# Weight sums on multiples of 128 bytes, plain chunks first and fifth, an eighth product group per layer in a decoder trunk

## The chip, the cores and the metric

The kernel runs on one core of a Trainium2 chip. The metric is the device time of one execution in microseconds (us). The engines that matter here are PE (TensorE, matrix products), DVE (VectorE) and ACT (ScalarE). Nearly all data lie in the on-chip memory SBUF, 128 partitions wide, and a tile's place is its byte offset within a partition. A difference of 0.2% is 4 us.

## The reference

The reference is a two-layer decoder trunk on 256 tokens of width 2048 in float32. What bears on the change is the feed-forward block, once in each layer:

```
D_MODEL = 2048
SEQ = 256
D_FF = ((8 * D_MODEL // 3 + 255) // 256) * 256   # 5632

def swiglu_ffn(x, g, w_in, w_out):
    h = rms_norm(x, g)
    gate, up = jnp.split(h @ w_in, 2, axis=-1)
    return x + (jax.nn.silu(gate) * up) @ w_out
```

Around it stand a recurrent block (layer 0) and a shared key/value projection with a sliding-window attention (layer 1), which the change leaves as they are but for where their tiles lie.

## The kernel before

**Three products for one.** Each float32 operand is held as two rounded parts, a high and a low one, and a product is the sum of high x high, high x low and low x high, each at PE's single-pass rate. Activations are held so in work tiles `s`; model weights arrive by DMA in `raw` (128 x 1024) and are split into `hi` (by ACT, line 311) and `lo` (by DVE, line 312). Four buffers of each rotate. One such tile is a *chunk*: 256 input features by 512 output features. `stream` (line 337) runs over all chunks: at chunk i it issues the load of chunk i+4, the split of chunk i+3, and the matmuls of chunk i.

**Stationary and moving.** A matmul first loads a 128 x 128 stationary operand into the array and then streams a moving operand of 256 or 512 columns past it. In the profile's rows `out<-in,in` the first input is the moving one and the second the stationary one.

**Direct groups.** `group` (line 362) takes 512 output features over all 2048 input features: 8 chunks of 24 matmuls on line 358, each with the model weight (`hi` or `lo`) stationary and 256 activation columns (`s`) moving: `b<-s,hi`. In the groups that are given `sync`, some chunks have three matmuls with 512 moving columns in place of six with 256.

**Fast groups.** A feed-forward block's input product has 22 groups (g = 0 to 21). Groups 0 to 4 are direct, and so are those from 18 on; groups 5, 7, ..., 17 (`FAST`) are *fast* ones, in `fast_group` (line 502), and the even ones between are direct. In a fast group the activations are stationary and the model weights move (`b<-hi,s`). Six of its eight chunks (`PAIRS`: 0, 1, 2, 4, 5, 6) are computed with seven block products in place of eight: 21 matmuls in place of 24. Three of the seven products use the weights as they are: 9 matmuls with `hi` or `lo` moving. The other four use sums of weight blocks, which `mix` (line 314) makes on DVE and ACT, three chunks ahead, in the work tiles `mh` and `ml`: 12 matmuls with a work tile moving, `b<-s,s`. The other two chunks are plain. Chunk 7 has 24 matmuls of 256 columns. Chunk 3 (`RUNS`) has nine of 512 and six of 256: three wide ones, a narrow one, three wide ones, a narrow one, three wide ones, four narrow ones. Ahead of chunk 3, `flush` issues what the fast group before left over: four transposes on line 711.

**The end of a block.** The group after the last fast one (g = 18) is direct with `sync` in chunks 0, 3, 4 and 5 and with the last flush ahead of chunk 3; behind it, a background task (`split`, in `ffn`) begins to split the 22 gated products into high and low parts for the output product, whose 88 chunks are all direct.

**What sets the order.** Each engine runs its instructions in the order of the program. A run-ahead planner (`run_bg`, with budgets in ns for DVE and ACT) only decides between which chunks the background pieces are issued.

**Where tiles lie.** All work tiles are of 4096 bytes and come from a rotating list of 30 (`whole`, `double`). Tiles are laid out in the order of their creation, each rounded up to 32 bytes: 16,384 bytes of DMA scratch, 128 bytes of constants, `par` (1096 bytes), `con` (4104), `cc` (128), `x`, `raw`, `hi`, `lo`, `t`, `h` (multiples of 1024), two `rstd` (1032 each), `acc`, two `sq` (1024 each), `zero` (1536), and then the work tiles. So `raw`, `hi` and `lo` begin at multiples of 128 bytes, and the two `rstd` (1056 bytes each with the rounding, 2112 together, which is 64 more than a multiple of 128) put all work tiles 64 bytes past such a multiple. In the following "at 0" and "at 64" stand for the offset modulo 128. All slices that a matmul takes begin a multiple of 512 bytes into their tile, so they are at 0 or 64 as the tile is.

Of the kernel before, what the change touches and what calls it, by code (L numbers as in the profile page):

```python
# [12 lines left out]
F32 = mybir.dt.float32  # L13
F32R = mybir.dt.float32r
# [3 lines left out]
P = 128  # L18
D = 2048
T = 256  # L20
# [15 lines left out]
K_ONE, K_BLK, K_SEL0, K_SEL1, K_ID = 0, 128, 256, 384, 512  # L36
K_HS, K_MASK = 640, 642
NCON = 642 + 384


class Val:
# [7 lines left out]
class Trunk:  # L49
# [10 lines left out]
    DEBT = 2500.0  # L60
    SYNC = (0, 2, 5)
    PLAIN = 4
    FAST = tuple(range(5, 18, 2))
    PAIRS = (0, 1, 2, 4, 5, 6)
    RUNS = 3
    OWED = 9000.0
    MORE = 2800.0
    WARM = 30
# [3 lines left out]
    def __init__(self, ctx, tc, dram):  # L72
        self.tc, self.nc, self.d = tc, tc.nc, dram
        nc = self.nc
        const = ctx.enter_context(tc.tile_pool(name="const", bufs=1))
        psum = ctx.enter_context(tc.tile_pool(name="psum", bufs=1, space=bass.MemoryType.PSUM))
        tmp = ctx.enter_context(tc.tile_pool(name="tmp", bufs=1))
        self.tmp = tmp
        self.par = const.tile([P, NPAR], F32, name="par")
        self.con = const.tile([P, NCON], F32, name="con")  # L80
        self.cc = const.tile([P, 32], F32, name="cc")
        self.x = [const.tile([P, 4, T], F32, name=f"x{i}") for i in range(4)]
        self.whole = deque((i, 0) for i in range(30))
        self.stamp = 0
        self.part = {F32: deque(), F32R: deque()}
        self.spool = const
        self.held = {}
        self.raw = [const.tile([P, 1024], F32, name=f"raw{i}") for i in range(4)]
        self.hi = [const.tile([P, 1024], F32R, name=f"hi{i}") for i in range(4)]
        self.lo = [const.tile([P, 1024], F32R, name=f"lo{i}") for i in range(4)]  # L90
# [4 lines left out]
        self.tmps = deque(const.tile([P, T], F32, name=f"t{i}") for i in range(4))  # L95
        self.halves = deque(const.tile([P, T], F32, name=f"h{i}") for i in range(4))
        self.rstd = [const.tile([P, T + 2], F32, name=f"rstd{i}") for i in range(2)]
        self.acc = const.tile([P, T], F32, name="acc")
        self.sq = deque(const.tile([P, T], F32, name=f"sq{i}") for i in range(2))
        self.zero = const.tile([P, P + T], F32R, name="zero")  # L100
# [41 lines left out]
        self.nc.vector.reciprocal(out, a)  # L142


    def double(self, dt=F32R):
        i, _ = self.whole.popleft()
        s = self.spool.tile([P, 4 * T], dt, tag=f"s{i}", name=f"s{i}")
        self.held[id(s)] = (i, s)
        return s

# [163 lines left out]
    def mix(self, i, raw, hi, lo):  # L314

        act, tt = self.nc.scalar.activation, self.nc.vector.tensor_tensor
        d = self.double(F32)
        mh, ml = self.double(), self.double()
        two = lambda ap: ap.rearrange("p (a c) -> p a c", c=T)
        q = slice(T, 4 * T)  # L320
        act(hi[:, q], raw[:, q], AF.Copy)  # L321
        tt(two(d[:, 0:2 * T]), two(raw[:, T:3 * T]), raw[:, 0:T].unsqueeze(1).to_broadcast([P, 2, T]), ALU.subtract)  # L322
        tt(d[:, 2 * T:3 * T], raw[:, 2 * T:3 * T], d[:, 0:T], ALU.add)
        tt(d[:, 3 * T:4 * T], raw[:, 3 * T:4 * T], d[:, 2 * T:3 * T], ALU.subtract)  # L324
        act(mh[:, :], d[:, :], AF.Copy)  # L325
# [179 lines left out]
    def fast_group(self, src, xn, mx, g, done, final):  # L505
# [10 lines left out]
        def plain(c, hi, lo):  # L516
# [732 lines left out]

    def run(self):  # L1250
        nc, d = self.nc, self.d
        const = self.tmp
        self.nm = const.tile([P, T + 2], F32, name="nm")
        self.nt = const.tile([P, T + 2], F32, name="nt")
        self.r2 = const.tile([P, 2], F32, name="r2")
        self.rrs = [const.tile([P, 48], F32, name=f"rr{i}") for i in range(2)]
# [90 lines left out]
```

## Time and profile before

| | |
|---|---|
| time, median of 3 runs | 1994.03 us (1992.72 to 1994.22) |
| the profiled execution | 1994.55 us, its span 1992.4 us |
| DVE, ACT busy | 1458.5 us (73%), 1123.0 us (56%) |
| DMA | 376.56 MB, mean 189 GB/s |
| granted PE clock | 1.00 in every stage |
| direct matmuls, line 358 | 12,807 |
| fast-group matmuls, line 512 | 2310: 1008 with a work tile moving, 1302 with `hi` or `lo` |

The profile comes from one profiled execution. "Busy" of PE is a union of modelled spans that overlap, so a PE that is busy all the time says only that it never ran dry, not that it goes at its best rate. That rate is read from the timeline: each row has the start of a run of like matmuls, the time to the end of its last, and their number, and the difference of the starts of two rows, divided by the number of matmuls between them, is the *pitch*, the time that one matmul takes in the stream.

### The profile page before, as it was taken

How to read it: one execution, taken by the hardware profiler on the slowest of the kernel's cores; microseconds unless marked ns; L12 is line 12 of the kernel's file. 1: busy time of each engine (PE TensorE's matmuls, PEld its weight loads, DVE VectorE, ACT ScalarE, POOL GpSimd, SP SyncE). 2: the span in 40 equal slices, each digit the busy share in tenths (PEclk: the TensorE clock that was granted, in tenths of full speed). 3: DMA queues.
4: the chain of work that ended last, by engine and by line, in shares of the span. 5: the costliest groups of instructions: out<-in, count | busy, mean ns of one | idle time of the engine just before them, and what ended most of it. 6: DMA issues, size and time to landing. Idle time of an engine off the chain costs nothing. (4 is left out here: it accounts for less than half of the span.)

```text
span 1992.4 us, 39949 instructions
## 1 busy us (share of the span) xinstructions
PE 1982.9 (100%) x16487; PEld 1935.5 (97%) x16487; DVE 1458.5 (73%) x2319; ACT 1123.0 (56%) x1626; POOL 0.2 (0%) x4
## 2 busy tenths in 40 slices
PE   9999999999999999999999999999999999999999
PEld 9999999999999999999998789999999999999999
DVE  8989868788888955555677776697888888444543
ACT  7788756555555744444556775564555556444342
POOL 0000000000000000000000000000000000000000
PEclk9999999999999999999999999999999999999999
DMA  7555655655566565555554334565655655556663
GB/s 267 194 188 180 201 191 180 202 198 194 199 201 199 196 196 197 191 191 201 192 181 154 111 128 150 189 191 190 203 201 196 198 196 197 187 190 204 208 202 128
DMA packets 105015, 376.56 MB, mean 189 GB/s; under 512 B 11648, under 2 KB 13824, under 8 KB 104832
## 3 DMA queue, kind: packets, MB, share of 16 engines
q1 hardware_dynamic: 104544, 373.60, 56.6%
q8 instruction: 129, 2.11, 0.4%
q14 instruction: 54, 0.44, 0.1%
q10 hardware_dynamic: 288, 0.40, 0.1%
HBM read 371.86 MB, written 2.10 MB: 188 GB/s over the span
## 5 line engine op out<-in xcount | busy, mean ns | idle before, releaser
L358 PE MATMUL b<-s,hi 128*128 128x256 f32 (+1 forms) x8455 | 1128.5, 280 | 1.6 <-ACT s L118 1.2
L312 DVE TENSOR_TENSOR lo<-raw,hi 128x1024 fp32r<-128x1024 f32 (+1 forms) x621 | 755.9, 1220 | 435.7 <-ACT hi L311 421.2
L358 PEld LDWEIGHTS b<-s,hi 128*128 128x128 f32 x8455 | 1051.7, 188 | 14.2 <-ACT s L118 2.0
L311 ACT ACTIVATE hi<-raw 128x1024 fp32r<-128x1024 f32 (+1 forms) x621 | 654.2, 1056 | 590.5 <-PE b L358 475.0
L358 PE MATMUL b<-s,lo 128*128 128x256 f32 x4352 | 647.1, 277 | 0.0
L358 PEld LDWEIGHTS b<-s,lo 128*128 128x128 f32 x4352 | 564.7, 188 | 0.1
L512 PE MATMUL b<-hi,s 128*128 128x256 f32 (+1 forms) x868 | 163.0, 292 | 0.0
L325 ACT ACTIVATE s<-s 128x1024 fp32r<-128x1024 f32 x84 | 89.2, 1062 | 108.6 <-DVE s L324 107.8
L512 PEld LDWEIGHTS b<-hi,s 128*128 128x128 f32 x868 | 130.4, 189 | 3.8
L512 PE MATMUL b<-s,s 128*128 128x256 f32 x1008 | 133.3, 281 | 0.0
L512 PEld LDWEIGHTS b<-s,s 128*128 128x128 f32 x1008 | 125.2, 189 | 0.0
L327 DVE TENSOR_TENSOR s<-s,s 128x1024 fp32r<-128x1024 f32 x84 | 102.7, 1222 | 20.1 <-ACT s L325 19.9
L512 PE MATMUL b<-lo,s 128*128 128x256 f32 (+1 forms) x434 | 114.1, 289 | 0.0
L118 ACT ACTIVATE s<-s 128x512 fp32r<-128x512 f32 (+3 forms) x172 | 83.0, 519 | 18.4 <-DVE s L127 13.1
L321 ACT ACTIVATE hi<-raw 128x768 fp32r<-128x768 f32 x84 | 70.3, 843 | 35.1 <-issue 21.8
L1232 PE MATMUL b<-hi,s 128*128 128x512 f32 x256 | 84.0, 408 | 0.0
L326 DVE TENSOR_TENSOR lo<-raw,hi 128x768 fp32r<-128x768 f32 x84 | 79.9, 951 | 0.0
L512 PEld LDWEIGHTS b<-lo,s 128*128 128x128 f32 x434 | 76.4, 188 | 1.8
L127 DVE TENSOR_TENSOR s<-s,s 128x512 fp32r<-128x512 f32 (+2 forms) x143 | 74.0, 549 | 4.4 <-ACT s L118 4.4
L322 DVE TENSOR_TENSOR s<-raw 128x512 f32<-128x512 f32 x84 | 57.7, 686 | 12.4 <-DMA raw<-in_ffn_in 12.3
L118 ACT ACTIVATE s<-b 128x256 fp32r<-128x256 f32 (+4 forms) x112 | 49.9, 480 | 25.9 <-PE b L1128 7.9
L1232 PEld LDWEIGHTS b<-hi,s 128*128 128x128 f32 x256 | 45.8, 189 | 9.6 <-issue 1.4
(117 smaller groups left out, 1098.6 us busy)
## 6 DMA issues: line engine op xcount, KB each, us to landing
raw<-in_ffn_in SPq DMA_DIRECT2D x352, 512.0 KB, 3.3
raw<-in_ffn_out SPq DMA_DIRECT2D x176, 512.0 KB, 3.3
raw<-in_lru_in SPq DMA_DIRECT2D x63, 512.0 KB, 3.8
raw<-in_lru_out SPq DMA_DIRECT2D x32, 512.0 KB, 3.4
raw<-in_w_q SPq DMA_DIRECT2D x32, 512.0 KB, 3.2
raw<-in_w_o SPq DMA_DIRECT2D x32, 512.0 KB, 3.3
raw<-in_gate SPq DMA_DIRECT2D x8, 512.0 KB, 4.0
raw<-in_kv SPq DMA_DIRECT2D x8, 512.0 KB, 3.2
```

The lines of the kernel that those rows point to most:

```text
L118: self.nc.scalar.activation(out, in_, func, **kw)
L127: self.nc.vector.tensor_tensor(out, a, b, op)
L311: self.nc.scalar.activation(hi[:, q], raw[:, q], AF.Copy)
L312: self.nc.vector.tensor_tensor(lo[:, q], raw[:, q], hi[:, q].bitcast(F32), ALU.subtract)
L321: act(hi[:, q], raw[:, q], AF.Copy)
L322: tt(two(d[:, 0:2 * T]), two(raw[:, T:3 * T]), raw[:, 0:T].unsqueeze(1).to_broadcast([P, 2, T]), ALU.subtract)
L325: act(mh[:, :], d[:, :], AF.Copy)
L326: tt(lo[:, q], raw[:, q], hi[:, q].bitcast(F32), ALU.subtract)
L327: tt(ml[:, :], d[:, :], mh[:, :].bitcast(F32), ALU.subtract)
L358: self.nc.tensor.matmul(ps[f][:, 0:c1 - c0], w, x2[k][:, c0:c1], start=f not in begun, stop=last and all(q[1] != f for q in todo[n + 1:]))
L512: nc.tensor.matmul(st["ps"][b][:, h % 2 * T:(h % 2 + n) * T], x, w, start=b not in st["begun"], stop=True, skip_group_check=True)
L1232: nc.tensor.matmul(st[g][b][:, :], x, q, start=c + kt == 0 and x is xh and q is wh, stop=c == 7 and kt == 1 and q is wl)
```

## The change

There are four edits.

- Groups 5, 7, ..., 19 are fast: eight in each layer. The groups behind (20, 21) are direct, and `sync`, the last flush and the start of `split` go with group 20.
- The plain chunks of a fast group are 0 and 4, both in the form with wide matmuls, and chunks 1, 2, 3, 5, 6, 7 use seven products. The flush stands ahead of chunk 4.
- The work tiles get 64 bytes more each, their list has 33, and `double` places a tile within them: `mh` and `ml` at 0, all others at 64, as before.
- The small tiles are laid out anew (a pad of 608 bytes, one more `sq` that serves as `acc`), and the DMA scratch is 2048 bytes.

```diff
+PAD = 152
...
-    FAST = tuple(range(5, 18, 2))
-    PAIRS = (0, 1, 2, 4, 5, 6)
-    RUNS = 3
+    FAST = tuple(range(5, 20, 2))
+    PAIRS = (1, 2, 3, 5, 6, 7)
+    RUNS = (0, 4)
...
-        self.whole = deque((i, 0) for i in range(30))
+        const.tile([P, PAD], F32, name="pad")
+        self.sq = deque(const.tile([P, T], F32, name=f"sq{i}") for i in range(3))
+        self.acc = self.sq.popleft()
+        self.whole = deque((i, 0) for i in range(33))
...
-    def double(self, dt=F32R):
+    def double(self, dt=F32R, place=64):
         i, _ = self.whole.popleft()
-        s = self.spool.tile([P, 4 * T], dt, tag=f"s{i}", name=f"s{i}")
+        o = (place // 64 + i) % 2 * 16
+        s = self.spool.tile([P, 4 * T + 16], dt, tag=f"s{i}", name=f"s{i}")[:, o:o + 4 * T]
...
-        mh, ml = self.double(), self.double()
+        mh, ml = self.double(place=0), self.double(place=0)
...
-            if c == self.RUNS:
+            if c in self.RUNS:
                 n = narrow(wide[3]) + narrow(wide[4]) + narrow(wide[5])
                 todo = sum(map(full, wide[0:3]), []) + n[0:1] + sum(map(full, wide[6:9]), []) + n[1:2]
                 todo += sum(map(full, wide[9:12]), []) + n[2:]
...
-                if c == self.RUNS:
+                if c == self.RUNS[1]:
                     self.flush()
...
-    nc = bacc.Bacc("TRN2", target_bir_lowering=False, num_devices=1)
+    nc = bacc.Bacc("TRN2", target_bir_lowering=False, num_devices=1, dynamic_dma_scratch_size=2048)
```

Two places on PE show the order. The first is where a direct group ends and the first fast group begins (`hi` and `lo` are of the chunk, `s` are work tiles, the outputs are PSUM banks). Before:

```order
L358 MATMUL b_86<-s_4432,hi_78 128x256 x2
L358 MATMUL b_86<-s_4432,lo_82 128x256
L512 MATMUL b_89<-hi_75,s_3900 128x256 x2
L512 MATMUL b_89<-lo_79,s_3900 128x256
L512 MATMUL b_88<-hi_75,s_3900 128x256 x2
L512 MATMUL b_88<-lo_79,s_3900 128x256
L512 MATMUL b_88<-hi_75,s_3929 128x256 x2
L512 MATMUL b_88<-lo_79,s_3929 128x256
L512 MATMUL b_90<-s_4742,s_3929 128x256 x2
L512 MATMUL b_90<-s_4743,s_3929 128x256
```

And with the change:

```order
L362 MATMUL b_103<-s_4397,hi_84 128x256 x2
L362 MATMUL b_103<-s_4397,lo_88 128x256
L516 MATMUL b_105<-hi_81,s_3898 128x512 x2
L516 MATMUL b_105<-lo_85,s_3898 128x512
L516 MATMUL b_104<-hi_81,s_3898 128x256
L516 MATMUL b_105<-hi_81,s_3898 128x512 x2
L516 MATMUL b_105<-lo_85,s_3898 128x512
L516 MATMUL b_104<-hi_81,s_3898 128x256
L516 MATMUL b_104<-hi_81,s_3898 128x512 x2
L516 MATMUL b_104<-lo_85,s_3898 128x512
L516 MATMUL b_104<-hi_81,s_3898 128x256 x2
L516 MATMUL b_104<-lo_85,s_3898 128x256 x2
```

The group now begins with the plain chunk in wide matmuls, and the first seven-product chunk, with its sums of weights, follows as the second.

The second place is around the flush in the second fast group (`con` holds the identity for the transposes). Before, the rows from the end of chunk 2 to the beginning of chunk 4:

```order
L512 MATMUL b_87<-s_5283,s_4028 128x256
L711 MATMUL b_85<-con,s_5064 128x128 x4
L512 MATMUL b_88<-hi_78,s_4144 128x512 x2
L512 MATMUL b_88<-lo_82,s_4144 128x512
L512 MATMUL b_87<-hi_78,s_4144 128x256
L512 MATMUL b_88<-hi_78,s_4144 128x512 x2
L512 MATMUL b_88<-lo_82,s_4144 128x512
L512 MATMUL b_87<-hi_78,s_4144 128x256
L512 MATMUL b_87<-hi_78,s_4144 128x512 x2
L512 MATMUL b_87<-lo_82,s_4144 128x512
L512 MATMUL b_87<-hi_78,s_4144 128x256 x2
L512 MATMUL b_87<-lo_82,s_4144 128x256 x2
```

With the change, the rows from the end of chunk 3:

```order
L516 MATMUL b_104<-s_5303,s_4059 128x256
L715 MATMUL b_102<-con,s_5053 128x128 x4
L516 MATMUL b_105<-hi_81,s_4174 128x512 x2
L516 MATMUL b_105<-lo_85,s_4174 128x512
L516 MATMUL b_104<-hi_81,s_4174 128x256
L516 MATMUL b_105<-hi_81,s_4174 128x512 x2
L516 MATMUL b_105<-lo_85,s_4174 128x512
L516 MATMUL b_104<-hi_81,s_4174 128x256
L516 MATMUL b_104<-hi_81,s_4174 128x512 x2
L516 MATMUL b_104<-lo_85,s_4174 128x512
L516 MATMUL b_104<-hi_81,s_4174 128x256 x2
L516 MATMUL b_104<-lo_85,s_4174 128x256 x2
```

The flush and the wide chunk are the same instructions in the same order as before; they have moved one chunk back, and three seven-product chunks stand ahead of them and three behind.

More of the change, by code (lines that the diff above doesn't have):

```diff
@@ L76, in __init__ @@
         psum = ctx.enter_context(tc.tile_pool(name="psum", bufs=1, space=bass.MemoryType.PSUM))
-        tmp = ctx.enter_context(tc.tile_pool(name="tmp", bufs=1))
-        self.tmp = tmp
         self.par = const.tile([P, NPAR], F32, name="par")
@@ L81, in __init__ @@
         self.cc = const.tile([P, 32], F32, name="cc")
-        self.x = [const.tile([P, 4, T], F32, name=f"x{i}") for i in range(4)]
-        self.whole = deque((i, 0) for i in range(30))
+        self.rstd = [const.tile([P, T + 2], F32, name=f"rstd{i}") for i in range(2)]
+        self.nm, self.nt = (const.tile([P, T + 2], F32, name=n) for n in ("nm", "nt"))
+        self.r2 = const.tile([P, 2], F32, name="r2")
+        self.rrs = [const.tile([P, 48], F32, name=f"rr{i}") for i in range(2)]
+        self.zero = const.tile([P, P + T], F32R, name="zero")
+        const.tile([P, PAD], F32, name="pad")
+        self.x = [const.tile([P, 4, T], F32, name=f"x{i}") for i in range(4)]
+        self.raw = [const.tile([P, 1024], F32, name=f"raw{i}") for i in range(4)]
+        self.hi = [const.tile([P, 1024], F32R, name=f"hi{i}") for i in range(4)]
+        self.lo = [const.tile([P, 1024], F32R, name=f"lo{i}") for i in range(4)]
+        self.tmps = deque(const.tile([P, T], F32, name=f"t{i}") for i in range(4))
+        self.halves = deque(const.tile([P, T], F32, name=f"h{i}") for i in range(4))
+        self.sq = deque(const.tile([P, T], F32, name=f"sq{i}") for i in range(3))
+        self.acc = self.sq.popleft()
+        self.whole = deque((i, 0) for i in range(33))
         self.stamp = 0
@@ L87, in __init__ @@
         self.held = {}
-        self.raw = [const.tile([P, 1024], F32, name=f"raw{i}") for i in range(4)]
-        self.hi = [const.tile([P, 1024], F32R, name=f"hi{i}") for i in range(4)]
-        self.lo = [const.tile([P, 1024], F32R, name=f"lo{i}") for i in range(4)]
         self.sets = [[psum.tile([P, 512], F32, name=f"b{4 * i + j}") for j in range(4)] for i in range(2)]
@@ L94, in __init__ @@
         self.started = False
[L95 to L100, printed above, removed]
         self.jobs = []
@@ L1251, in run @@
         nc, d = self.nc, self.d
[L1252 to L1256, printed above, removed]
         self.rv = {i: Val() for i in range(4)}
```

## The prediction

> **What bounds the kernel now.** I read the page's busy times first, then those of single stages, then the PE timeline.
>
> ```profile
> PE 1982.9 (100%) x16487; PEld 1935.5 (97%) x16487; DVE 1458.5 (73%) x2319; ACT 1123.0 (56%) x1626; POOL 0.2 (0%) x4
> ```
>
> PE is busy throughout. The stages below are one fast group with its flush, the direct group behind it, and the output product of the last layer; the columns are the stage, its length, and busy PE, PEld, DVE, ACT and POOL, then granted clock and DMA.
>
> ```profile
> 452.19:472.99 20.80, 20.80 (x172) 20.40 (x171) 17.49 (x25) 11.91 (x16) 0.00 (x0) 1.00 0.63 207
> 472.99:494.75 21.76, 21.76 (x195) 21.76 (x193) 18.97 (x27) 11.30 (x12) 0.00 (x0) 1.00 0.56 190
> 1755.00:1992.00 237.00, 234.36 (x2044) 233.16 (x2042) 109.64 (x105) 89.79 (x89) 0.00 (x0) 1.00 0.57 187
> ```
>
> PE never runs dry in the groups, the granted clock is 1.00, and DVE, the next engine, has 36.46 us of work in a pair of groups of 42.56 us. So the time is the number of matmuls times their pitch. A direct group of 192 matmuls takes 21.76 us, 113 ns each.
>
> The pitch is not one number. The key/value stage alternates twelve direct matmuls (line 1038, work tile at 64 moving, weights at 0 stationary) with twelve in the roles of a fast group (lines 1047 to 1049, weights moving). These are the starts of five such dozens:
>
> ```profile
> 1012.94 0.39 PE L1038 MATMUL b<-s,hi 128*128 128x256 f32 x2
> ...
> 1014.30 0.28 PE L1047 MATMUL b<-hi,s 128*128 128x256 f32 x1
> ...
> 1015.72 0.40 PE L1038 MATMUL b<-s,hi 128*128 128x256 f32 x2
> ...
> 1017.13 0.28 PE L1047 MATMUL b<-hi,s 128*128 128x256 f32 x1
> ...
> 1018.50 0.39 PE L1038 MATMUL b<-s,hi 128*128 128x256 f32 x2
> ```
>
> The differences over 12 are 113, 118, 118 and 114 ns. The shapes are the same, so the stream has two states, **short** (113) and **long** (118). The step from direct to fast roles turned short into long, then long into short; the step from fast to direct roles kept the state both times.
>
> Now a fast group's beginning: nine matmuls with `hi`/`lo` moving, twelve with weight sums, the next nine, the next twelve.
>
> ```profile
> 452.19 0.40 PE L512 MATMUL b<-hi,s 128*128 128x256 f32 x2
> ...
> 453.25 1.59 PE L512 MATMUL b<-s,s 128*128 128x256 f32 x12
> 454.68 0.41 PE L512 MATMUL b<-hi,s 128*128 128x256 f32 x2
> ...
> 455.72 1.58 PE L512 MATMUL b<-s,s 128*128 128x256 f32 x12
> ```
>
> 1.06/9 = 118, 1.43/12 = 119, 1.04/9 = 116. The direct group ahead was short, so the group starts long, as in the key/value stage. The twelve, whose two operands both lie at 64, cost 119, and behind them the stream is nearly short. So the sums are slow by some 6 ns each, and they also **pull the stream out of the long state**.
>
> Then the flush, the plain chunk with wide matmuls, and the chunk behind it:
>
> ```profile
> 459.60 0.60 PE L711 MATMUL b<-con,s 128*128 128x128 f32 x4
> 459.95 0.71 PE L512 MATMUL b<-hi,s 128*128 128x512 f32 x2
> ...
> 462.83 0.40 PE L512 MATMUL b<-hi,s 128*128 128x256 f32 x2
> ...
> 463.89 1.59 PE L512 MATMUL b<-s,s 128*128 128x256 f32 x12
> ```
>
> The flush takes 0.35 us, the wide chunk 2.88, and the nine behind it 1.06, 118 ns each: the wide chunk leaves the stream **long**. That it does so from the short state too is seen where the attention's wide matmuls, in the same roles, follow three short ones:
>
> ```profile
> 1035.74 0.28 PE L1047 MATMUL b<-hi,s 128*128 128x256 f32 x1
> ...
> 1036.08 0.62 PE L1232 MATMUL b<-hi,s 128*128 128x512 f32 x2
> 1036.55 0.39 PE L1232 MATMUL b<-lo,s 128*128 128x512 f32 x1
> 1036.78 0.63 PE L1232 MATMUL b<-hi,s 128*128 128x512 f32 x2
> ```
>
> 0.34/3 = 113, and the next three wide ones take 0.70 us. In a direct group wide matmuls do something else:
>
> ```profile
> 1749.56 2.04 PE L358 MATMUL b<-s,hi 128*128 128x512 f32 x13
> 1751.44 1.10 PE L358 MATMUL b<-s,lo 128*128 128x256 f32 x8
> 1752.38 2.05 PE L358 MATMUL b<-s,hi 128*128 128x256 f32 x16
> 1754.27 1.10 PE L358 MATMUL b<-s,lo 128*128 128x256 f32 x8
> 1755.21 2.00 PE L358 MATMUL b<-s,hi 128*128 128x256 f32 x13
> 1757.04 1.07 PE L358 MATMUL b<-s,lo 128*128 128x256 f32 x8
> 1757.95 1.98 PE L358 MATMUL b<-s,hi 128*128 128x256 f32 x16
> ```
>
> Both rows of 13 hold three wide ones. Behind the first the pitch is still 0.94/8 = 118; behind the second 0.91/8 = 114. So wide matmuls can end the long state, or fail to. In the second row one narrow at 118 and nine at 113 leave 1.83 - 0.12 - 1.02 = 0.69 us for the three. Left alone, a direct group stays long:
>
> ```profile
> 1681.72 2.05 PE L358 MATMUL b<-s,hi 128*128 128x256 f32 x16
> ...
> 1698.68 2.05 PE L358 MATMUL b<-s,hi 128*128 128x256 f32 x16
> ```
>
> 16.96 us for six chunks of 24: 117.8 ns, with no way back by itself. At that pitch a direct group takes 22.62 us, 0.86 more than 21.76.
>
> **The change part by part.**
>
> *Weight sums at 0.* All 21 matmuls of a seven-product chunk then have the weights moving at 0 and the activations stationary at 64. The 6 ns of a conflict go, but so does what ended the long state. What is late next is the long state itself: the price per matmul is not shown for such a chunk, and lies between 113 (short) and 119 (as now). I take 117.8, the row of a stream left alone in the long state, because the chunk ahead leaves it there.
>
> *Plain chunks first and fifth, both wide.* The first chunk stands where the stream comes from a direct group; no row shows wide matmuls there. Bounds for it: three times 0.69 and six at 113, 2.75 us; and 2.88 as above with a restart in it. I take 2.81: three times the 0.70 of the attention's three wide ones, and six narrow ones at 0.118. It ends long in my forecast. The fifth chunk is the same instructions behind the same flush as the fourth is now, so 0.35 + 2.88 us, and it ends long.
>
> A fast group is then 2.81 + 6 x 21 x 0.1178 (14.84) + 0.35 + 2.88 = 20.88 us, against 20.80. Fourteen groups: **+1.1**.
>
> *Direct groups behind fast ones.* Today a fast group ends short, as its successor's 21.76 us show. With the change its last three chunks are long, the step to direct roles keeps the state, and these groups have no wide matmuls. Layer 0 has seven of them (6 to 18), layer 1 six (6 to 16); its group 18 is mostly long already, counted at nothing (at most +0.86). 13 x 0.86 = **+11.2**.
>
> *An eighth fast group per layer.* In layer 0 it replaces a short direct group: 20.88 - 21.76 = -0.88. In layer 1 it replaces group 19, the one in the rows from 1681.72 that is long: 20.88 - 22.62 = -1.74. Together **-2.6**.
>
> *Costed at nothing.* The sums of the eighth group, and the splits of the gated products, which begin two direct groups later, are DVE work. The cover is the 14% of a pair that DVE is idle, and the output product, where it is busy 109.64 of 237 us; if it failed, rival F gives the price. New places of small tiles and longer rows of work tiles concern DVE and ACT, under the same cover. Three more work tiles only loosen waits, and PE has none in these stages. The smaller DMA scratch is bounded by loads that are issued four chunks (10.9 us) ahead. Other stages keep their PE order, but a restart there may fall into the other state: four groups' worth either way, 3.5 us.
>
> **Sum**: 1.1 + 11.2 - 2.6 = +9.7 us. From the profiled execution's 1994.55 (its span is 1992.4, the rest lies around it and is not touched) that is 2004.2; the median of the runs is 0.5 below that execution, so I predict **2003.7 us** (+0.5%).
>
> **The rivals.**
>
> *B, the short state everywhere.* The wide chunks bring the stream to the short state, as one did at 1755.21, and with all sums at 0 nothing takes it away. Then a fast group is 2.75 + 126 x 0.1133 (14.28) + 0.35 + 2.88 = 20.26 us, 0.54 less; 14 x -0.54 = -7.6; the eighth groups give -1.5 and -2.36: -11.4 us, **1982.6**. It decides at the last three wide matmuls of the chunk. For it: the row at 1755.21, and that two wide chunks are placed where the long state begins. Against it: 462.83 to 463.89, where the same chunk failed, and 1036.08, where the roles are those of a fast group.
>
> *C1, only the fifth chunk succeeds.* Three chunks long (63 x 0.1178 = 7.42), three short (63 x 0.1133 = 7.14), direct groups short: 2.81 + 7.42 + 0.35 + 2.88 + 7.14 = 20.60; 14 x -0.20 - 1.16 - 2.02 = -6.0: **1988.0**. *C2, only the first succeeds*: 2.75 + 7.14 + 0.35 + 2.88 + 7.42 = 20.54; 14 x -0.26 - 1.22 - 2.08 + 11.2 = +4.3: **1998.3**. Against both speaks the same row as against B, for C2 less, since its chunk follows direct matmuls and no restart.
>
> *D, the step back to direct roles ends the long state.* The 11.2 fall away: -1.5, **1992.5**. The key/value rows speak against it, though twice only.
>
> *E, places do not matter*: the twelve cost 119 for another reason, and the states stay as they are. Only the eighth groups remain: 20.80 - 21.76 and 20.80 - 22.62, -2.8 us, **1991.2**. The 119 beside 113 for equal shapes speaks against it.
>
> The Trainium skill's page "SBUF — State Buffer", section "SBUF: two separate sides", would have it so: it gives PE a port for the moving operand and a second, independent one for the weight load, and says that PE never waits on anyone. By that rule the sum would be E's. The trace does not agree: 119 against 113 ns with the same shapes, and two pitches for identical instructions.
>
> *F, DVE becomes the bound* at the last direct group, where the 22 splits now begin late. Between 0 and the whole of DVE's idle share there (2.8 us of 21.76) per layer would go to PE waits beyond the forecast: 2003.7 to **2009**. The 14% that DVE is idle speak against it.
>
> *That the sums are not at 0* is excluded by the layout: the work tiles are 4160 bytes apart, 64 more than a multiple of 128, and `double` adds 0 or 64 by the tile's number, so `mh` and `ml` alternate to the same side.
>
> **How the numbers follow.** Forecast A 0.54; B 0.15; C1 0.08; C2 0.08; D 0.09; E 0.04; F 0.02. Faster by over 0.2% (about the least that a measurement of this kernel can tell from no change) are B and C1, 0.23; within it D and E, 0.13; slower A, C2 and F, 0.64. A's own range is 2000 to 2008: 3.5 for the other stages, 0.86 for group 18. The range for 8 in 10 must go beyond it to C2, D, E and C1, and leaves out B and the end of F: 1985 to 2008.
>
> **What would show it.** Right: in the changed profile the 126 matmuls of the seven-product chunks at 118 ns, the nine and the twelve alike; direct groups 6 to 18 of 22.6 us; fast groups near 20.9. B: nine and twelve alike at 113, fast groups of 20.3, direct groups of 21.8. C1 and C2: a change of pitch at the fifth chunk. D: 118 in the fast groups, 21.8 in the direct ones. E: twelve still at 119 behind nine at 114. F: PE idle in group 21 with DVE as releaser. The forecast is wrong if a first or fifth chunk is followed by 113 ns.

## The result, and the profile after

The changed kernel takes 2018.57 us (median of four runs, 2017.38 to 2018.66), the one before 1993.38 beside it (four runs): ratio 1.0129, 95% interval 1.0111 to 1.0146. It is slower, as forecast, but by 25 us where the forecast had 9.7, outside its range. The span went from 1992.4 to 2016.8 us at the same granted clock of 1.00.

```profile
PE 2007.0 (100%) x16297; PEld 1952.9 (97%) x16297; DVE 1488.0 (74%) x2379; ACT 1139.0 (56%) x1640; POOL 0.2 (0%) x4
```

This is the busy line of the page after. PE is still the engine that never runs dry, and DVE did not move up to it (74% against 73%). So the 24.4 us are pitch again, or they are nowhere. The next lines are a fast group with its flush and the direct group behind it (columns as in the prediction's windows):

```profile
460.24:480.80 20.56, 20.56 (x163) 19.79 (x161) 17.92 (x25) 12.69 (x17) 0.00 (x0) 1.00 0.56 186
480.80:502.89 22.09, 22.09 (x195) 22.09 (x193) 19.25 (x28) 11.45 (x13) 0.00 (x0) 1.00 0.61 209
```

The forecast had 20.88 and 22.62 here. Both came out shorter, and neither is a stream in one state: 22.09 lies between 21.76 (short) and 22.62 (long). The loss is elsewhere. Four stages of layer 0, first before, then after: the output product of the recurrent block, groups 0 to 4, groups 5 to 19 (the stretch of the fast groups), and the output product of the feed-forward block.

```profile
212.03:299.17 87.14, 87.14 (x735) 85.64 (x734) 63.48 (x100) 49.56 (x77) 0.00 (x0) 1.00 0.60 199
299.17:410.05 110.88, 110.82 (x933) 109.03 (x931) 92.40 (x158) 63.73 (x84) 0.00 (x0) 1.00 0.58 190
410.05:729.98 319.93, 319.93 (x2710) 316.63 (x2708) 270.10 (x369) 179.99 (x218) 0.00 (x0) 1.00 0.60 198
773.50:1012.94 239.44, 239.44 (x2079) 237.97 (x2077) 130.19 (x151) 109.70 (x134) 0.00 (x0) 1.00 0.59 194
```

```profile
213.66:304.03 90.37, 90.37 (x734) 88.74 (x733) 63.63 (x101) 49.86 (x78) 0.00 (x0) 1.00 0.58 192
304.03:417.98 113.95, 113.95 (x932) 112.17 (x931) 91.34 (x155) 64.20 (x85) 0.00 (x0) 1.00 0.56 185
417.98:737.15 319.17, 319.17 (x2622) 312.90 (x2621) 274.07 (x378) 179.55 (x210) 0.00 (x0) 1.00 0.60 197
782.64:1027.25 244.61, 244.61 (x2078) 243.03 (x2077) 129.62 (x150) 109.67 (x134) 0.00 (x0) 1.00 0.58 190
```

The stretch that holds every edit of the order changed by -0.8 us (in layer 1 by +2.6, from 321.14 to 323.77). The three stages whose matmuls the change does not touch lost 3.2, 3.1 and 5.2. Cut in this way from end to end, the fast stretches of both layers give +1.9 of the 24.4 us, and all other stages +22.5. (Times of a stage run from its first matmul to the first of the next.) What differs there is where the tiles lie, and with it the number of work tiles and the size of the DMA scratch; run 4 has these last two and none of the loss.

The output product shows how. This is the PE timeline after, within one run of direct chunks:

```profile
852.08 2.05 PE L362 MATMUL b<-s,hi 128*128 128x256 f32 x16
...
854.91 2.05 PE L362 MATMUL b<-s,hi 128*128 128x256 f32 x16
...
857.74 2.03 PE L362 MATMUL b<-s,hi 128*128 128x256 f32 x13
859.61 1.10 PE L362 MATMUL b<-s,lo 128*128 128x256 f32 x8
860.55 1.98 PE L362 MATMUL b<-s,hi 128*128 128x256 f32 x16
...
863.27 1.98 PE L362 MATMUL b<-s,hi 128*128 128x256 f32 x16
...
865.99 2.05 PE L362 MATMUL b<-s,hi 128*128 128x256 f32 x16
```

A row of 16 whose last matmul ends after 2.05 us is long, after 1.98 us short: 852.08 to 854.91 is 2.83 us for 24 matmuls, 118 each, and 860.55 to 863.27 is 2.72, 113 each. The state changes at 852.08, 860.55 and 865.99, each time at the first matmul of a chunk, and the row of 13 at 857.74, which holds three wide ones, does not end it. What the trace does not say is where the work tiles lie; that follows from the program. With rows of 4160 bytes and the 64 that `double` adds or not, work tile 0, 1, 2, 3, ... lies at 64, 64, 192, 192, 64, ... **modulo 256**; modulo 128 all of these are 64, which is all that the prediction looked at. (`hi` and `lo` lie at 0 modulo 256, the sums at 0 or 128.) In the kernel before every work tile lies at 192, and `hi` and `lo` at 128. Around the rows above, the chunk ahead of 852.08 reads a work tile at 64, the one from 852.08 reads one at 192, two at 64 from 854.91, two at 192 from 860.55, and from 865.99 on at 64. Matched with the program over the whole trace, and taking only switches with at least eight direct matmuls of 256 columns on either side: from 192 to 64 the stream went from short to long 66 times and stayed long 29 times, and it was short after none; from 64 to 192 it went from long to short 72 times, stayed long 18 times, and went from short to long 11 times. At one place it hardly turns: of the 279 stretches of 16 or more such matmuls at one place, one holds a change, and PE paused in that one.

The fast group shown above has the sign by which the prediction called itself wrong, a wide chunk with 113 ns behind it:

```profile
463.02 0.39 PE L516 MATMUL b<-hi,s 128*128 128x256 f32 x2
...
464.04 1.58 PE L516 MATMUL b<-s,s 128*128 128x256 f32 x12
```

The nine behind the first plain chunk take 1.02 us, 113 each. By the program, the wide matmuls of all 16 plain chunks in layer 0 have `hi` at 0 and a work tile at 192, and all 16 leave the stream short; in layer 1 all 16 have the work tile at 64, and all leave it long.

### The profile page after: what moved, and what is told of

Same layout as the page of the kernel before. It is cut to its first block, busy times and chain, and to the rows that moved or that the text cites. A ratio compares the mean times of both kernels' runs of the same rounds, so it can differ in the third digit from the quotient of the medians.

```text
span 2016.8 us, 39609 instructions
## 1 busy us (share of the span) xinstructions
PE 2007.0 (100%) x16297; PEld 1952.9 (97%) x16297; DVE 1488.0 (74%) x2379; ACT 1139.0 (56%) x1640; POOL 0.2 (0%) x4
## 5 line engine op out<-in xcount | busy, mean ns | idle before, releaser
L362 PE MATMUL b<-s,hi 128*128 128x256 f32 (+1 forms) x8199 | 1114.9, 282 | 1.1 <-ACT s L121 1.0
L316 DVE TENSOR_TENSOR lo<-raw,hi 128x1024 fp32r<-128x1024 f32 (+1 forms) x609 | 742.0, 1221 | 435.6 <-ACT hi L315 418.1
L362 PEld LDWEIGHTS b<-s,hi 128*128 128x128 f32 x8199 | 1036.6, 188 | 14.2 <-ACT s L121 1.7
L516 PE MATMUL b<-hi,s 128*128 128x256 f32 (+1 forms) x896 | 186.3, 305 | 0.0
L329 ACT ACTIVATE s<-s 128x1024 fp32r<-128x1024 f32 x96 | 101.8, 1060 | 89.4 <-DVE s L328 89.1
L516 PE MATMUL b<-s,s 128*128 128x256 f32 x1152 | 150.5, 280 | 0.0
L516 PEld LDWEIGHTS b<-s,s 128*128 128x128 f32 x1152 | 141.6, 188 | 0.0
L331 DVE TENSOR_TENSOR s<-s,s 128x1024 fp32r<-128x1024 f32 x96 | 117.4, 1222 | 22.4 <-ACT s L329 22.4
L516 PE MATMUL b<-lo,s 128*128 128x256 f32 (+1 forms) x448 | 130.7, 303 | 0.0
L130 DVE TENSOR_TENSOR s<-s,s 128x512 fp32r<-128x512 f32 (+3 forms) x144 | 74.5, 551 | 4.4 <-ACT s L121 4.4
```

The costliest lines, as they stand in the source:

```text
L130: self.nc.vector.tensor_tensor(out, a, b, op)
L316: self.nc.vector.tensor_tensor(lo[:, q], raw[:, q], hi[:, q].bitcast(F32), ALU.subtract)
L362: self.nc.tensor.matmul(ps[f][:, 0:c1 - c0], w, x2[k][:, c0:c1], start=f not in begun, stop=last and all(q[1] != f for q in todo[n + 1:]))
L516: nc.tensor.matmul(st["ps"][b][:, h % 2 * T:(h % 2 + n) * T], x, w, start=b not in st["begun"], stop=True, skip_group_check=True)
```

## The experiments

Runs 1 to 4 set two theories against each other. **R** (the rows): rows of 4160 bytes spread the work tiles over two places modulo 256, and this costs in all direct matmuls. **L** (the long state): the loss is the long state that the wide chunks leave, as forecast. From run 5 on, R is split in two. **S** (the switch): a change of place modulo 256 from one work tile to the next turns the state. **P** (the place): one of the two places is itself slow. Later runs ask what puts the fast groups in one state or the other. Each run has the kernel before beside it on the same chip, but the runs are spread over several chips, so runs are compared by their ratios. Runs 2, 4 and 5 also have the smaller DMA scratch, and run 4 shows that it costs nothing.

**1. The changed kernel with all work tiles at one place.** Rows of 4352 bytes (17 x 256) put all work tiles at 192 and all sums at 128; the pad puts `hi` and `lo` at 128.

```diff
-PAD = 152
+PAD = 184
-        self.whole = deque((i, 0) for i in range(33))
+        self.whole = deque((i, 0) for i in range(31))
-        o = (place // 64 + i) % 2 * 16
-        s = self.spool.tile([P, 4 * T + 16], ...)
+        o = place // 64 * 16
+        s = self.spool.tile([P, 4 * T + 64], ...)
```

> The changed kernel with work tiles of 4352 bytes (17 x 256) in place of 4160, 31 of them, so that all work tiles lie at 192 modulo 256 and the weight sums at 128, as hi and lo do. Theory R (rows of 4160 bytes spread the work tiles over two places modulo 256, and that costs in all direct matmuls): the loss goes, 1983 to 1993 us. Theory L (the long state that the wide chunk leaves, as forecast): 2000 to 2008 us, with fast groups of 20.9 us and direct groups behind them of 22.6.

Measured: 2001.84 us, ratio 1.0049 (1.0033 to 1.0065), four runs. This is in L's range and not in R's, since R left out the loss that the forecast had; the forecast was 2003.7. The four stages:

```profile
211.14:298.27 87.13, 87.13 (x734) 85.65 (x733) 63.49 (x100) 49.56 (x77) 0.00 (x0) 1.00 0.59 199
298.27:408.84 110.57, 110.51 (x933) 108.74 (x931) 90.58 (x155) 63.46 (x84) 0.00 (x0) 1.00 0.57 190
408.84:733.93 325.09, 325.09 (x2623) 318.57 (x2621) 274.28 (x379) 181.05 (x211) 0.00 (x0) 1.00 0.59 195
778.33:1017.77 239.44, 239.44 (x2078) 237.97 (x2077) 129.09 (x147) 109.70 (x134) 0.00 (x0) 1.00 0.58 194
```

The three stages outside are back at the lengths of the kernel before, and the loss is where the forecast put it, in the fast stretch. A fast group with the direct group behind it, and the PE timeline of its last seven-product chunks:

```profile
582.47:603.37 20.90, 20.90 (x163) 20.09 (x161) 17.43 (x24) 12.35 (x15) 0.00 (x0) 1.00 0.61 201
603.37:625.99 22.62, 22.62 (x195) 22.62 (x194) 19.56 (x28) 11.38 (x13) 0.00 (x0) 1.00 0.59 190
```

```profile
598.42 0.40 PE L516 MATMUL b<-hi,s 128*128 128x256 f32 x2
...
599.48 1.58 PE L516 MATMUL b<-s,s 128*128 128x256 f32 x12
600.89 0.40 PE L516 MATMUL b<-hi,s 128*128 128x256 f32 x2
```

1.06/9 and 1.41/12 are both 118: the nine and the twelve alike, and 20.90 and 22.62 us where the forecast worked out 20.88 and 22.62. Modulo 512 these rows alternate too (4352 is 8.5 x 512), and nothing turns outside the fast stretches: the relevant place is the one modulo 256.

**2. The kernel before with the longer rows** (its order of work, seven fast groups, sums placed as the other tiles):

```diff
-        s = self.spool.tile([P, 4 * T], dt, tag=f"s{i}", name=f"s{i}")
+        o = i % 2 * 16
+        s = self.spool.tile([P, 4 * T + 16], ...)[:, o:o + 4 * T]
```

> The kernel before with work tiles of 4160 bytes, all of them at 64 modulo 128 as before (sums too), but at 64 or 192 modulo 256 by number. Nothing else but the smaller DMA scratch. Theory R: 2015 to 2025 us, direct matmuls at 117 ns on the mean. Theory L: no change, 1993 us.

Measured: 2025.8 us, 1.0169 (1.0153 to 1.0185). R's range ends 0.8 us below this, and L's "no change" is refuted. The longer rows alone cost 33 us, more than the whole change. The output product of layer 0 takes 245.46 us in it where it took 239.44. Here `hi` and `lo` lie at 128, and the directions of the switch are exchanged: from 64 to 192 the stream was long after all 119 switches (61 from short), and from 192 to 64 it went from long to short 67 times of 117. So what counts is not the place 64 or 192, but how the moving tile lies to the weights.

**3 and 4. Layout and order apart.** The third run is the changed kernel with the old order (seven fast groups, plain chunks 3 and 7, only 3 wide), the fourth the kernel before with the new order and 33 work tiles of 4096 bytes.

```diff
-    FAST = tuple(range(5, 20, 2))
-    PAIRS = (1, 2, 3, 5, 6, 7)
-    RUNS = (0, 4)
+    FAST = tuple(range(5, 18, 2))
+    PAIRS = (0, 1, 2, 4, 5, 6)
+    RUNS = (-1, 3)
```

(The fourth run has these lines the other way round, with `RUNS = (0, 4)`, in the kernel before.)

> The changed kernel with the groups and the chunk order of before (seven fast groups, plain chunks fourth and eighth): the layout alone. Theory R: 2018 to 2024 us, the whole loss. Theory L: at most 2000 us, since no wide chunk stands first.

> The kernel before with eight fast groups, plain chunks first and fifth, and 33 work tiles: the order alone, the old places. Theory R: 1989 to 1993 us (two direct groups replaced, 2.8 us). Theory L: the sums still pull the stream out, 1990 to 1995 us. It gives the price of the order.

Measured: the new layout with the old order 2024.85 us, 1.0164 (1.0146 to 1.0182); the new order with the old layout 1988.99 us (ten runs), 0.9984 (0.9975 to 0.9994). The third is 0.85 us above R's range and far above L's, the fourth at the lower edge of R's and below L's. The order is a gain of some 3 us where its sums stay at 192; the layout is a loss of 32. (Together they cost 25, so the two do not simply add.)

**5. The kernel before with all work tiles at 64** modulo 256, `hi` and `lo` still at 128. S expects no loss here, P a large one.

```diff
         self.zero = const.tile([P, P + T], F32R, name="zero")
+        const.tile([P, 32], F32, name="pad")
```

> The kernel before with all work tiles moved by 128 bytes, so that all lie at 64 modulo 256 and none changes its place (and the smaller DMA scratch). Theory S (it is the change of place from one work tile to the next that throws the stream into the long state): 1990 to 1995 us as before. Theory P (64 modulo 256 is a bad place, 192 a good one): nearly all direct matmuls long, 12,800 x 4 ns, 2040 us or more.

Measured: 2028.87 us, 1.0194 (1.0177 to 1.0211). A miss for both: there is no switch in it, yet it loses 38 us (2028.87 against 1990.4 beside it), less than P asked for. Its output product of layer 0, and rows of the timeline within it:

```profile
785.63:1034.12 248.49, 248.49 (x2078) 246.86 (x2077) 130.32 (x152) 109.94 (x135) 0.00 (x0) 1.00 0.56 187
```

```profile
847.61 2.04 PE L359 MATMUL b<-s,hi 128*128 128x512 f32 x13
849.49 1.11 PE L359 MATMUL b<-s,lo 128*128 128x256 f32 x8
850.43 2.05 PE L359 MATMUL b<-s,hi 128*128 128x256 f32 x16
...
853.25 2.04 PE L359 MATMUL b<-s,hi 128*128 128x256 f32 x13
855.13 1.10 PE L359 MATMUL b<-s,lo 128*128 128x256 f32 x8
```

The rows of 13 have the three wide matmuls that in the kernel before ended the long state (the prediction's rows at 1755.21). Here they leave it as it is (0.94/8 = 118 behind them). Matched with the program over all direct groups where the state can be told on both sides, a chunk with three wide matmuls met the short state 9 times and set the long one each time; it met the long state 62 times and left it so 55 times. In the kernel before and run 1 together, it met the short state 112 times and left it so 108 times, and of 30 times in the long state it ended 17. So what wide matmuls do hangs on how the two operands lie to each other: with the moving tile 64 bytes ahead of the stationary one modulo 256 (192 and 128) they hold the short state and often bring it, with it 64 behind (64 and 128) they bring or leave the long one. In a fast group the roles are exchanged, and the relation decides there too: with `hi` at 128 moving past a work tile at 192, 64 behind, all 32 wide chunks of run 1 leave the stream long, as do the 16 of layer 1 in the changed kernel (0 and 64), while the 16 of its layer 0 (0 and 192, which is 64 ahead modulo 256) leave it short.

**6. Without any wide matmul in the direct groups**, once in the changed kernel and once in the kernel before.

```diff
-    SYNC = (0, 2, 5)
+    SYNC = ()
-  ... (0, 3, 4, 5) if end else (), True, 3 if end else None)
+  ... (), True, 3 if end else None)
```

> The changed kernel with no wide matmuls in the direct groups (the wide first and fifth chunks stay). Theory S (each change of place between work tiles throws the stream into another state by itself): 2012 to 2025 us, direct matmuls at 117 ns on the mean. Theory W (the spread of places only makes the wide matmuls of the direct groups fail or harm): 1995 to 2003 us.

> The kernel before with no wide matmuls in the direct groups, the control of e11. Nothing ends a long state there but the sums: slower than before, 1998 to 2030 us, with long stretches at 118 ns and no change of pitch inside a stretch without a restart or a change of roles.

Measured: the changed kernel 2024.73 us, 1.0157 (1.0138 to 1.0176); the kernel before 2028.85 us, 1.0176 (1.0158 to 1.0194). The first is in S's range and outside W's, the second in the range expected of it. In the second one the output product of layer 0, its first row and one near its end are:

```profile
785.03:1033.78 248.75, 248.75 (x2115) 248.75 (x2114) 128.49 (x146) 107.99 (x129) 0.00 (x0) 1.00 0.57 187
```

```profile
785.03 2.05 PE L358 MATMUL b<-s,hi 128*128 128x256 f32 x16
...
1028.12 2.05 PE L358 MATMUL b<-s,hi 128*128 128x256 f32 x16
```

88 chunks of 24 are 2112 matmuls, and 248.75/2112 is 117.8 ns: with one place and no wide ones, nothing changes the state over the whole stage. The 239.44 us of the kernel before are the same stage held short by its wide matmuls; they are worth 36 us in the kernel, most of them outside the fast stretches. (Run 5 lost about as much, with the wide matmuls there but 64 behind.) In the first of the two kernels the stream does change, with no wide matmul near:

```profile
801.83 1.98 PE L362 MATMUL b<-s,hi 128*128 128x256 f32 x16
...
804.56 2.05 PE L362 MATMUL b<-s,hi 128*128 128x256 f32 x16
...
815.86 1.98 PE L362 MATMUL b<-s,hi 128*128 128x256 f32 x16
```

By the program, the work tile is at 192 from 801.83, at 64 from 804.56, at 192 again from 815.86. So the switch itself turns the state, though not each time: over this whole trace, from 64 to 192 it went from long to short 52 times and stayed long 62 times, and from 192 to 64 it went from short to long 36 times and was short after none of 104. In 241 stretches of 16 or more direct matmuls at one place, four hold a change, and PE paused in each of these. That much of S holds; that there is no loss without a switch fell with run 5. In the changed kernel the output product is 244.61 us, some 56% of the way from 239.3 (2112 at 113.3) to 248.8 (at 117.8).

**7. Which of the two wide chunks sets the long state.** From the kernel of run 1, with the first plain chunk in narrow matmuls, and with both:

```diff
-            if c in self.RUNS:
+            if c == self.RUNS[1]:      # first narrow
+            if c < 0:                  # both narrow
```

> e1 with the first plain chunk of a fast group in 24 matmuls of 256 columns, the fifth still with wide ones. If the wide matmuls set the long state there: a group entered from a long direct group turns short with the change of roles and stays so for four chunks, 0.37 us less per group, 1995 to 1998 us. If the change of roles alone sets the long state: 2002 us as e1.

> e1 with both plain chunks narrow, no wide matmuls in the fast groups. If the wide matmuls set the long state in the fifth chunk, groups and direct groups turn short: 1983 to 1990 us. If the restart behind the flush sets it: as e7, 1995 to 1998 us, or 2002 us if neither.

Measured: first narrow 1997.71 us, 1.0042 (1.0027 to 1.0057); both narrow 1986.31 us (ten runs), 0.9981 (0.9971 to 0.999). The fast stretch of layer 0 in the first (410.23 on) and the second:

```profile
410.23:732.85 322.62, 322.62 (x2694) 319.34 (x2693) 273.91 (x377) 180.22 (x209) 0.00 (x0) 1.00 0.59 196
```

```profile
409.21:726.48 317.27, 317.27 (x2767) 317.27 (x2765) 273.21 (x377) 179.01 (x209) 0.00 (x0) 1.00 0.59 199
```

Both are in the ranges expected if the wide matmuls set the long state. 325.09, 322.62, 317.27: the wide matmuls of the fast groups cost 7.8 us in a layer, 15.6 us in all (2001.84 - 1986.31 is 15.5, on two chips). With the first chunk narrow, the step from a long direct group to a fast one turns the stream short for 87 matmuls (113.5), and the wide chunk behind the flush makes it long again. The turn that the prediction had read off two steps from direct to fast roles is there at all 32 beginnings of a fast group in these two kernels: short became long, or long became short.

**8. Ways to the short state.** From run 1: the sums of chunks 1 and 5 at 192, where the work tiles are, so that they pull the stream out of the long state (`jobs` now carries the number of the chunk).

```diff
-        mh, ml = self.double(place=0), self.double(place=0)
+        o = 64 if self.jobs[i][2] in (1, 5) else 0
+        mh, ml = self.double(place=o), self.double(place=o)
```

> The changed kernel with rows of 4352 bytes (e1), but the sums of chunks 1 and 5 at 192 modulo 256 like the other work tiles; those of chunks 2, 3, 6 and 7 stay at 128 with hi and lo. If conflicting sums end the long state, and sums at the place of hi and lo then leave the short one alone: chunks 2, 3, 6, 7 at 113 ns, direct groups short, 1983 to 1988 us. If the sums do not do that: 2002 us as e1.

> e6 once more, on the same chip as the run above: a ratio of 0.996 to 0.999 to the kernel before, and above that of the run above by 0.001 to 0.003 if the first chunk's sums in front are worth their price.

Measured: 1985.16 us (ten runs), 0.9977 (0.9968 to 0.9986), and on another chip, beside the last run below, 1984.61, 0.9968 (0.9955 to 0.998). Both are as expected. The PE timeline of the second:

```profile
591.90 1.59 PE L517 MATMUL b<-s,s 128*128 128x256 f32 x12
593.33 0.40 PE L517 MATMUL b<-hi,s 128*128 128x256 f32 x2
...
594.37 1.52 PE L517 MATMUL b<-s,s 128*128 128x256 f32 x12
595.73 0.39 PE L517 MATMUL b<-hi,s 128*128 128x256 f32 x2
...
598.11 1.98 PE L363 MATMUL b<-s,hi 128*128 128x256 f32 x16
```

The twelve with both operands at 192 cost 1.43/12 = 119, the nine behind them 1.04/9 = 116, then the twelve at 128 1.36/12 = 113, and the direct group starts short. All 32 pulls of this trace end so.

Then two runs that keep both plain chunks narrow: one pull, in chunk 1; and the plain chunks put at 3 and 7, the flush at 3, with the sums of chunk 0 at 192 and its four sum products ahead of the other three. (The number that `jobs` carries is the chunk's in the first of these kernels, the chunk's plus one in the second.)

```diff
+        o = 64 if self.jobs[i][2] == 1 else 0
...
-    PAIRS = (1, 2, 3, 5, 6, 7)
-    RUNS = (0, 4)
+    PAIRS = (0, 1, 2, 4, 5, 6)
+    RUNS = (0, 3)
...
+            if c == 0:
+                todo = todo[3:] + todo[:3]
```

> e8 (rows of 4352 bytes, no wide matmuls in the fast groups) with the sums of chunk 1 at 192 modulo 256, in conflict with the activations; the other sums at 128. If these sums end the long state that the change of roles leaves, chunks 2 and 3 turn short, 0.2 us per group: 1981 to 1984 us. If not: 1986 us as e8.

> e8 with the plain chunks fourth and eighth as in the kernel before (flush ahead of the fourth, both narrow), and in the first chunk the four products with sums ahead of the three others, those sums at 192 modulo 256, all other sums at 128. Twelve conflicting matmuls at 119 ns then stand where the roles change, and all behind them is short: 20.35 us a group against 20.66 in e8, 1979 to 1983 us. If sums in front do not end the long state: 1986 us or more.

Measured: 1988.01 us, 0.9975 (0.9961 to 0.999), and 1987.13, 0.9971 (0.996 to 0.9981), nine runs each. Both are misses: by their ratios neither is better than both narrow without a pull (0.9981) beyond the intervals. The second one's PE timeline behind two flushes, 43.4 us apart, shows why:

```profile
585.68 0.72 PE L517 MATMUL b<-hi,s 128*128 128x256 f32 x4
...
586.47 0.63 PE L517 MATMUL b<-hi,s 128*128 128x256 f32 x4
...
587.18 0.63 PE L517 MATMUL b<-hi,s 128*128 128x256 f32 x4
...
629.84 0.62 PE L517 MATMUL b<-hi,s 128*128 128x256 f32 x4
...
630.52 0.62 PE L517 MATMUL b<-hi,s 128*128 128x256 f32 x4
```

The same instructions at the same places: 0.71/6 = 118 behind the first flush, 0.68/6 = 113 behind the second. It is not chance either: in both layers of this trace the flushes leave the stream short and long strictly by turns, 8 short and 6 long of 14, while all 14 of the kernel with both narrow leave it short. What sets this is not shown. Each of the six long ones makes the rest of its group and the direct group behind it long. So the last run gives chunk 4, the first seven-product chunk behind the flush, a pull as well (`in (1, 5)` in place of `== 1`).

> e10 with the sums of the fifth chunk, the first seven-product chunk behind the flush, at 192 modulo 256 as well. If the restart behind the flush is a lottery between the two states and that is what kept e9 and e10 from their price, conflicting sums behind it make all direct groups short: 1980 to 1984 us on a chip where the kernel before takes 1993, a ratio of 0.993 to 0.996. If the restart is not what is left: 1987 us as e10, ratio 0.997.

Measured: 1982.01 us (five runs, 1981.15 to 1984.8), the kernel before 1990.41 beside it: 0.9958 (0.9944 to 0.9971), as expected. It is faster than the kernel before and the changed one; the repeat beside it, 0.001 above, is at the lower edge of what was expected, so what putting the sums in front is worth is hardly above the noise. Its fast stretch, and the pull behind a flush:

```profile
408.77:723.95 315.18, 315.18 (x2766) 315.18 (x2765) 272.86 (x376) 176.28 (x211) 0.00 (x0) 1.00 0.59 200
```

```profile
586.03 0.63 PE L517 MATMUL b<-hi,s 128*128 128x256 f32 x4
...
586.74 0.63 PE L517 MATMUL b<-hi,s 128*128 128x256 f32 x4
...
588.51 1.59 PE L517 MATMUL b<-s,s 128*128 128x256 f32 x12
589.94 0.40 PE L517 MATMUL b<-hi,s 128*128 128x256 f32 x2
...
590.98 1.30 PE L517 MATMUL b<-s,s 128*128 128x256 f32 x10
```

Behind the restart the stream was long (0.71/6 = 118), the twelve sums cost 119, the nine behind them 116 and falling. The flushes leave the stream long in the same six groups as in the kernel ahead of this one, so the restarts did not change, but every direct group between two fast groups now starts short.

## Why the prediction failed in size

**The two states and that they last** were right. Run 6 has 2112 matmuls of 117.8 ns in a row.

**The fast stretch** was right as a mechanism where all work tiles lie at one place (run 1), but not in the changed kernel. *A fast group of 20.88, direct groups of 22.62*: 20.90 and 22.62 in run 1, the two fast stretches together +9.1 us (2 x 325.09 against 319.93 + 321.14) where the sum had +9.7, and 2001.84 us in all for 2003.7. *The wide chunk leaves the stream long*: run 7 shows it for the places of run 1, 15.6 us for both layers; in the changed kernel it held in layer 1 only, and in layer 0, where `hi` lies 64 ahead of the work tile modulo 256, all 16 wide chunks left the stream short. *The sums pull the stream out of the long state while they lie where the work tiles lie, and not elsewhere*: the first kernel of run 8 against run 1. *The step from fast to direct roles keeps the state*: run 1, so rival D falls.

**The step that failed** stands under "Costed at nothing": "New places of small tiles and longer rows of work tiles concern DVE and ACT, under the same cover", and the bound of 3.5 us for the other stages. Longer rows concern PE. They put the work tiles at two places modulo 256, and the layout had been read modulo 128 only, where they are one. (The same reading stands in the step on the sums "at 0": they lie at 0 and at 128 by turns.) Run 2 shows the edit alone, +33 us; run 1 takes it out and is back at the forecast; the two kernels of run 6 show the state turn at the switch with no wide matmul near, and stand still without one. The missing term is the +22.5 us of the stages outside the fast stretches. The same two places also break up the long stretches that the forecast had in the fast part, which is why that part came out at +1.9: 24.4 is neither the forecast plus a term nor a larger price of the same term. That the kernel came out slower, as forecast, is then luck in the main: of the 9.7 us that the forecast had in the fast stretches, 1.9 are there.

**The rivals.** B (short everywhere, 1982.6) did not happen, though its step did in layer 0, where both wide chunks of every fast group brought the short state; it did not last through the groups, in which the work tiles lie at both places. Where `hi` lies 64 behind, the wide matmuls that B rested on are what makes the stream long. Run 8's last kernel comes close to the state that B described, without wide matmuls in the fast groups; that its 1982.01 us are so near B's time is chance, since the kernel before took 1990.41 beside it. C1 and C2 fall, since in no layer of the changed kernel or run 1 did one of the two wide chunks succeed and the other fail. E, that places do not matter, is refuted by run 2 and by run 5. The Trainium skill's page "SBUF — State Buffer", section "SBUF: two separate sides", by which E would have held, says that PE never waits on anyone; the trace shows no wait either, but 239.44 and 248.49 us for the same 88 chunks of instructions (before, and run 5) by 128 bytes of shift. F, DVE as the bound, did not show: in run 1 the pitch alone accounts for the fast stretch (8 x 20.90 + 7 x 22.62 = 325.5 for 325.09), with PE busy throughout.

**Open.** What happens inside PE or the memory in the two states was not found; the rows show that there are two and some of what turns them. Why the flushes of run 8's narrow kernels end by turns in the one and in the other is open. The 22.5 us, however, do not divide into switches and wide matmuls that fail. Outside the fast stretches (the span less the two stretches) the kernel before takes 1351.3 us, and 1384.9 without the wide matmuls of its direct groups (run 6); the changed kernel takes 1373.8, and 1377.9 without them. At one place the wide matmuls save 33.6 us, at two places 4.1. Without them the two places cost nothing; these stages are even 7 us shorter with two than with one. So what the two places cost is the work of the wide matmuls: a short state that these bring no longer lasts.

## What to carry to other kernels

In a kernel like this one, give tiles that matmuls read a row length that is a multiple of 256 bytes, so that all tiles of one kind have one place modulo 256. Then choose that place by a run, since one place alone is not enough (run 5, with all work tiles at 64, lost 38 us), and count an edit to a tile's size or to the layout as an edit to PE. Where equal matmuls have two pitches, find what turns the state, in the rows just before it turns, before changing the order of work; and test a layout change apart from an order change, since here the one cost 32 us and the other gained 3.

## What the hardware showed that was not expected

- A stream of 128 x 128 by 256 matmuls that never waits runs at 113.3 or at 117.8 ns per matmul, at a granted clock of 1.00, and stays in its state for at least 2112 matmuls (run 6). With both operands at the same place modulo 256 it takes 118 to 120 ns, and all 32 dozens of such matmuls in the repeat of run 8's first kernel brought a long stream back to the short state within the next nine.
- A change of the moving tile's place from 192 to 64 modulo 256, with the weights at 0, left the stream long 95 times of 95; the change back left it short 72 times of 101. With the weights at 128 (run 2) the directions are exchanged: long 119 times of 119 from 64 to 192, short 67 times of 117 from 192 to 64.
- Three wide matmuls (512 columns) in a direct chunk kept the short state 108 times of 112, and ended the long one 17 times of 30, with the moving operand 64 bytes ahead of the stationary one modulo 256 (the kernel before and run 1). With it 64 behind (run 5) they ended the short state 9 times of 9 and left the long one 55 times of 62. Run 5 as a whole lost 38 us.
- Behind four transposes, identical instructions at identical places went on at 118 ns once and at 113 ns 43 us later (run 8), by turns through all 14 flushes of that trace.
